# Squared norms of q taken per head behind q's convolution in place of per chunk in the chunk preparation (a DeltaNet and retention block on one core)

## The chip, the core and the metric

The kernel runs on one core of a Trainium2 chip. The core has four compute engines with a queue of their own each: PE (TensorE, matrix products and transposes), DVE (VectorE), ACT (ScalarE) and POOL (GpSimd); a fifth, SP (SyncE), issues DMA transfers, which ACT and POOL issue as well. Each engine works through its own list of instructions in order, and waits on semaphores for data of the others. The metric is the time of one execution on the device in microseconds (us).

## The reference

One layer over 256 context tokens and 1024 latent tokens of width 1024. The input is normalized and modulated, one projection gives the columns of two groups of four heads (a gated DeltaNet, group A, and a retention, group B), the heads' outputs are normalized, gated and projected back, and a SwiGLU follows. The change concerns the norm of q in group A:

```python
def l2_normalize(t):
    return t * lax.rsqrt(jnp.sum(t * t, axis=-1, keepdims=True) + NORM_EPS)
...
    p = (h @ w_in).astype(f32)
...
    qkv_a = jnp.concatenate([short_conv(qkv_a[:, :CTX_LEN], cw), short_conv(qkv_a[:, CTX_LEN:], cw)], axis=1)
    q, k, v = [t.reshape(b, tl, N_HEADS_GDN, HEAD_DIM) for t in jnp.split(qkv_a, 3, axis=-1)]
    q = l2_normalize(q) * (HEAD_DIM ** -0.5)
    k = l2_normalize(k)
...
    o_f = gated_delta_rule(q, k, v, g_f, jax.nn.sigmoid(b_f))
    o_b = to_bwd(gated_delta_rule(to_bwd(q), to_bwd(k), to_bwd(v), to_bwd(g_b), to_bwd(jax.nn.sigmoid(b_b))))
    o_gdn = rms_norm(o_f + o_b, gdn_norm_g) * jax.nn.silu(z.reshape(b, tl, N_HEADS_GDN, HEAD_DIM))
```

The convolution has five taps along the tokens and ends in a SiLU. The output of the delta rule is linear in q, so the kernel leaves q unnormalized and puts the norm into the RMS norm of the output: it needs |q|² for every latent token and head, and only there.

## The kernel before, in words

Tokens are cut into ten tiles of 128 (two of context, t = 0 and 1, and eight latent); heads of group A are 128 wide. All matrix products of the projections are done as three products of a split into high and low parts (`hhi`, `hlo`, `whi`, `wlo`). The order of stages is this.

- *Token-major projections* (`token_major(g, ...)`, matmuls in L371 to L373, bank `tm`): one group g of 256 columns, all tiles in pairs. What comes out goes through one operation (`res`, for rg a SiLU, L532) and to DRAM (`rd`, `zd`, L387).
- *k*, and then *q*: for each of four heads `conv_block` makes the projection with the channels on partitions (L611 to L613, bank `b`, name `b2`), copies it out on ACT (L614, L615), adds the other four taps on DVE (L621) and takes the SiLU on ACT (L624). The head's result `y` (128 channels x 1280 tokens, three buffers) is stored to `kd` or `qd`. For k, `kstat` also transposes each tile of y and sums its squares on ACT (L638). For q only the store follows.
- *rg* is `token_major(6)` and `token_major(7)`.
- *Chunk preparation* `pre(t)`: it loads a tile of k (`kc`) and, for t >= 2, of q (`qc`), both with four heads; takes k kT (`kk`) and, for latent tiles, transposes qc (`qt`, bank `pb`), sums the squares of the transposes into `nq` on ACT (L712), and takes k qT (`kq`). For both directions d it loads a row of decay sums (`gw`, from the product `gr`, L504), masks it on POOL (`e`, L722), takes exponentials on ACT (L726) and multiplies on DVE to `ut` (L730) and `sp` (L732).
- *Inversion* `invert(b)`: 32x32 blocks of three batches of tiles ([0,1,2,9], [3,8,4,7] and [5,6]) are inverted in 31 steps on DVE and POOL (L765 to L767); ACT and DVE copy the blocks to L (L758, L759) first. `merge(b)` joins the blocks with small matmuls (`m`).
- *v*: the same convolution for four heads, then transposes (`vT`), scaled on ACT into `vt` (L859, two buffers) and stored in `sd`.
- The *scan* over tiles in both directions follows; each step and direction loads one `pk` (128 x 3072, 1.5 MB) from `sd`, and has products `kS`, `Tr`, `up` and `o` on PE. Two steps stand ahead of the last projections, the others are interleaved with the retention, which begins with the loads `rdl`, `jcol`, `dist` and `vg` on SP. `gate` uses nq at the end of each tile's scan. Output projection and SwiGLU end the program.

Code order is not the order of execution: a scheduler fixes, when the program is built, the order of each engine's list, and instructions of several stages are mixed in it, as far as buffers allow. So v's first convolutions, the inversions and rg stand between the pieces of the chunk preparation.

PSUM banks are in three pools: `pa` (`tm`, `vT`), `pb` (`kt`, `qt`, `kk`, `kq`, `m`; three banks) and `pc` (the convolutions; two banks).

Of the kernel before, what the change touches and what calls it, by code (L numbers as in the profile page):

```python
# [11 lines left out]
AF = mybir.ActivationFunctionType  # L12
# [5 lines left out]
P = 128  # L18
D = 1024
KT = D // P  # L20
NCTX = 256
# [4 lines left out]
H = 4  # L26
# [12 lines left out]
def build(nc, tc, ap, dbg=None, stop=None, marks=None):  # L39
    root = ExitStack()  # L40
    V, S, G, T, SY = nc.vector, nc.scalar, nc.gpsimd, nc.tensor, nc.sync
# [24 lines left out]
    def checkpoint(name):  # L66
        if dbg is not None:
            marks.append((name, int(nc.cur_bb.bb.instructions[-1].name.split("-")[-1])))
        if stop == name:
            raise Stop()  # L70
# [16 lines left out]
    def bank(tag, name):  # L87
        return PS["pool"].tile([P, 512], F32, tag=tag, name=name, bufs=PS["tags"][tag])
# [4 lines left out]
    def bank_b(name):  # L93
        return bank("pb", name)
# [6 lines left out]
    def const(name, shape):  # L101
        t = C.tile(shape, F32, tag=name, name=name)
        S.dma_start(t, ap[name])
        return t
# [86 lines left out]
    try:  # L191

        cc = const("cc", [P, KT, 2])
        ident = const("ident", [P, P])
# [37 lines left out]
        W2 = None  # L232
# [127 lines left out]
        def tm_weights(g, kh, pl, q=S):  # L360
            return weights(ap["wt"][g, :, 4 * kh:4 * kh + 4, :], [4, 256], V, pl, q, raws.get((g, kh)), g == 0)

        def tm_bank(g):
            return bank_a("tm")[:, 0:WIDE if g == 0 else 256]
# [24 lines left out]
        def token_major(g, tiles, finish, store, pl, q=S):  # L389

            w = [tm_weights(g, kh, pl, q) for kh in range(2)]

            for p in range(0, len(tiles), 2):
                pair = [(t, tm_bank(g)) for t in tiles[p:p + 2]]
                for kh in range(2):
                    for t, o in pair:
                        tm_half(o, w[kh], kh, t)
                for t, o in pair:
                    tm_store(g, t, o, finish, store, pl)
# [47 lines left out]
        W2 = pool("w2", bufs=2)  # L447
# [86 lines left out]
        LAT, ALL = list(range(2, TT)), list(range(2, TT)) + [0, 1]  # L534
# [9 lines left out]
        nq = GS.tile([P, LT, H], F32, tag="nq", name="nq")  # L544
# [81 lines left out]
        def newy():  # L626
            return CV.tile([P, NTOK], F32, tag="y", name="y", bufs=3)
# [27 lines left out]
        for h in range(H):  # L655
            y = newy()
# [17 lines left out]
        sv = rsqrt(GS, nkf, TT * H, "sv")  # L674
        V.tensor_tensor(sv, sv, nkf, ALU.mult)
        sv3 = sv.rearrange("p (t h) -> p t h", h=H)
        for h in range(H):
            y = newy()
            conv_block(h, y, True)
            if h < 2:  # L680
                ada_rest(5, h)
            S.dma_start(qd[:, :, h, :].rearrange("t p j -> p t j"),
                        y[:, NCTX:].rearrange("p (t j) -> p t j", j=P))

        checkpoint("q")
        for g in (6, 7):
            token_major(g, LAT, fin_gate, S, W2, SY)
        checkpoint("rg")
        close(R2)
        close(W2)  # L690
# [9 lines left out]
        def pre(t):  # L700
# [4 lines left out]
                T.matmul(pk[:, h * P:(h + 1) * P], kc[:, h, :], kc[:, h, :], start=True, stop=True)  # L705
            if t >= 2:
                qc = load(GP, qd[t - 2], "qc", 2)
                pn = bank_b("qt")
                for h in range(H):
                    T.transpose(pn[:, h * P:(h + 1) * P], qc[:, h, :], ident)  # L710
                for h in range(H):
                    S.activation(pn[:, h * P:(h + 1) * P], pn[:, h * P:(h + 1) * P], AF.Square, accum_out=nq[:, t - 2, h:h + 1])  # L712
                pq = bank_b("kq")
                for h in range(H):
                    T.matmul(pq[:, h * P:(h + 1) * P], kc[:, h, :], qc[:, h, :], start=True, stop=True)
# [134 lines left out]
        for h in range(H):  # L850
            y = newy()
# [14 lines left out]
        for t in BATCH[2]:  # L866
            pre(t)
# [390 lines left out]
        for i, l in enumerate(pairs):  # L1258
            y = nxt
# [395 lines left out]
```

## Time and profile before

| what | us |
|---|---|
| three runs, in order of size | 1477.37, 1479.93, 1480.02 |
| the profiled execution's own time | 1477.96 |
| its span in the trace | 1476.2 |
| PE, DVE, ACT, POOL busy in the span | 1397.2, 964.6, 614.0, 590.3 |

The page of the profile begins with busy time by engine, then gives the span in 40 slices, the DMA queues, the chain of work that ended last, and the costliest groups of instructions. Of such a group the columns are line, engine and operation, out<-in with partitions x elements, and the count; then busy us and mean ns of one, and the idle time ahead of them on their engine with what ended most of it. The timeline has start, duration, engine (SPq and ACTq are these engines' DMA issues), and in brackets the idle time before with its releaser. A busy PE is not PE at its peak, since matmuls are pipelined: the step from one start to the next tells what one costs. Line numbers are those of the kernel before; the same line stands 10 further down in the changed kernel behind the added function.

### The profile page before, as it was taken

What the parts mean: (1) busy time and instruction counts of PE and PEld (TensorE: products, weight loads), DVE (VectorE), ACT (ScalarE), POOL (GpSimd) and SP (SyncE); (2) the same over time, 40 slices, a digit from 0 to 9 for tenths busy, and PEclk for the clock granted to TensorE, in tenths of its full rate; (3) what the DMA queues carried; (4) which work ended last, traced back from release to release, by engine and by line L of the source; (5) the groups of instructions that cost most, each with busy time, mean ns of one, the idle gap of its engine ahead of it and who ended that gap; (6) DMA issues with size and microseconds to landing.
All of it is one profiled execution on the core that took longest, in us unless ns stands there. A gap on an engine that the chain in (4) does not pass through costs nothing.

```text
span 1476.2 us, 24111 instructions
## 1 busy us (share of the span) xinstructions
PE 1397.2 (95%) x8919; PEld 1199.2 (81%) x8919; DVE 964.6 (65%) x1856; ACT 614.0 (42%) x1326; POOL 590.3 (40%) x501
## 2 busy tenths in 40 slices
PE   7999999986789999899799899999999999999997
PEld 2898888975689999898688688877888888788885
DVE  6566789289792435689676877556555564657477
ACT  5643564587333111245443623233333332444445
POOL 0120010243202344234144688898555552335321
PEclk9999999998899999999899999999999999999999
DMA  9536686688888625996532265674222242776863
GB/s 337 197 105 205 189 249 200 219 264 277 282 216 277 238 76 178 416 341 209 184 125 104 97 238 210 242 264 162 105 97 105 107 151 79 260 260 194 288 216 114
DMA packets 170421, 298.14 MB, mean 202 GB/s; under 512 B 43496, under 2 KB 93880, under 8 KB 165952
## 3 DMA queue, kind: packets, MB, share of 16 engines
q1 hardware_dynamic: 118752, 253.17, 50.2%
q10 hardware_dynamic: 49072, 35.83, 7.8%
q0 software_dynamic: 2480, 7.60, 1.4%
q8 instruction: 70, 1.15, 0.3%
q14 instruction: 47, 0.39, 0.1%
HBM read 206.60 MB, written 89.96 MB: 201 GB/s over the span
## 4 chain that ended last, share of the span: by engine, by line
PE 55%; POOL 6%; DMA 5%; DVE 4%; issue 2%; ACT 2%; SPq 1%; ACTq 0%; POOLq 0%; DVEq 0%
PE ffn L1344 7%; PE ffn L1342 6%; PE ffn L1343 6%; PE fo L1470 4%; PE fo L1469 4%; PE fo L1468 4%; PE tm L371 3%; PE tm L373 3%; PE tm L372 3%; PE op L1203 2%; PE op L1201 2%; PE op L1202 2%; DMA wd<-tw 2%; POOL ws L1315 1%; DMA pk<-sd 1%
## 5 line engine op out<-in xcount | busy, mean ns | idle before, releaser
L371 PE MATMUL tm<-whi,hhi 128*128 128x256 f32 (+1 forms) x704 | 199.5, 287 | 7.7 <-ACT vt L859 3.4
L372 PE MATMUL tm<-wlo,hhi 128*128 128x256 f32 (+1 forms) x704 | 199.3, 285 | 2.4 <-issue 2.0
L373 PE MATMUL tm<-whi,hlo 128*128 128x256 f32 (+1 forms) x704 | 197.7, 285 | 0.0
L371 PEld LDWEIGHTS tm<-whi,hhi 128*128 128x128 f32 x704 | 132.8, 190 | 11.8 <-ACT vt L859 3.6
L1342 PE MATMUL ffn<-t,whi 128*128 128x512 f32 x352 | 136.9, 390 | 1.3 <-ACT whi L344 1.3
L1344 PE MATMUL ffn<-t,wlo 128*128 128x512 f32 x352 | 137.0, 390 | 1.0 <-DVE wlo L345 1.0
L1343 PE MATMUL ffn<-t,whi 128*128 128x512 f32 x352 | 137.0, 389 | 0.0
L372 PEld LDWEIGHTS tm<-wlo,hhi 128*128 128x128 f32 x704 | 133.7, 190 | 2.1 <-issue 0.9
L373 PEld LDWEIGHTS tm<-whi,hlo 128*128 128x128 f32 x704 | 132.8, 190 | 2.6 <-issue 1.8
L344 ACT ACTIVATE whi<-wraw 128x512 fp32r<-128x512 f32 (+2 forms) x98 | 75.1, 771 | 141.4 <-PE ffn L1343 80.5
L344 ACT ACTIVATE whi<-ws 128x512 fp32r<-128x512 f32 x88 | 55.6, 632 | 171.5 <-PE ffn L1343 123.4
L345 DVE TENSOR_TENSOR wlo<-ws,whi 128x512 fp32r<-128x512 f32 x88 | 93.9, 1068 | 47.0 <-ACT whi L344 46.8
L1469 PE MATMUL fo<-wlo,ahi 128*128 128x512 f32 x308 | 120.2, 390 | 2.1 <-DVE wlo L345 2.1
L1468 PE MATMUL fo<-whi,ahi 128*128 128x512 f32 x308 | 119.3, 390 | 0.7 <-ACT ahi L344 0.7
L1470 PE MATMUL fo<-whi,alo 128*128 128x512 f32 x308 | 119.0, 390 | 0.0
L345 DVE TENSOR_TENSOR wlo<-wraw,whi 128x512 fp32r<-128x512 f32 (+2 forms) x92 | 99.4, 1082 | 24.6 <-ACT whi L344 24.6
L1342 PE MATMUL ffn<-b,whi 128*128 128x512 f32 x264 | 103.8, 393 | 4.4 <-ACT whi L344 4.4
L1344 PE MATMUL ffn<-b,wlo 128*128 128x512 f32 x264 | 103.6, 393 | 0.8 <-DVE wlo L345 0.8
L1343 PE MATMUL ffn<-b,whi 128*128 128x512 f32 x264 | 103.4, 392 | 0.0
L612 PE MATMUL b<-hlo,whi 128*128 128x512 f32 (+1 forms) x256 | 94.4, 369 | 0.0
L613 PE MATMUL b<-hhi,wlo 128*128 128x512 f32 (+1 forms) x256 | 94.3, 368 | 0.0
L611 PE MATMUL b<-hhi,whi 128*128 128x512 f32 (+1 forms) x256 | 94.3, 368 | 0.0
(446 smaller groups left out, 3448.1 us busy)
## 6 DMA issues: line engine op xcount, KB each, us to landing
adaw<-ada SPq DMA_DIRECT2D x48, 512.0 KB, 4.4
pk<-sd SPq DMA_DIRECT2D x16, 1536.0 KB, 10.0
wraw<-wfi SPq DMA_DIRECT2D x44, 512.0 KB, 3.7
ar<-ad SPq DMA_DIRECT2D x33, 512.0 KB, 4.7
w<-wfo SPq DMA_DIRECT2D x22, 512.0 KB, 5.7
wd<-tw SPq DMA_DIRECT2D x11, 1024.0 KB, 4.8
ad<-act SPq DMA_DIRECT2D x20, 512.0 KB, 3.0
raw<-wd SPq DMA_DIRECT2D x20, 512.0 KB, 4.9
```

The costliest lines, as they stand in the source:

```text
L344: S.activation(hi, raw, AF.Copy)
L345: e.tensor_tensor(lo, raw, hi.bitcast(F32), ALU.subtract)
L371: T.matmul(o, hhi[:, k, tsl], whi[:, k % 4, :], start=(k == 0), stop=False)
L372: T.matmul(o, hhi[:, k, tsl], wlo[:, k % 4, :], start=False, stop=False)
L373: T.matmul(o, hlo[:, k, tsl], whi[:, k % 4, :], start=False, stop=(k == KT - 1))
L612: T.matmul(o, whi[:, k, :], hl, start=False, stop=False)
L1342: T.matmul(o, whi[:, k, :], xhi(xn, slice(0, 4), k), start=(first and k == 0), stop=False, **kw)
L1343: T.matmul(o, whi[:, k, :], xlo(xn, slice(0, 4), k), start=False, stop=False, **kw)
L1344: T.matmul(o, wlo[:, k, :], xhi(xn, slice(0, 4), k), start=False, stop=(k == 3), **kw)
L1468: T.matmul(po[g][i], ahi[:, ts], whi, start=(j == 0 and not kw), stop=False, **kw)
L1469: T.matmul(po[g][i], ahi[:, ts], wlo, start=False, stop=False, **kw)
L1470: T.matmul(po[g][i], alo[:, ts], whi, start=False, stop=(j == FH - 1), **kw)
```

## The change

The transposes of q and the sums of their squares leave `pre(t)` and go into a new function `qstat(h, y)`. It works on a head at a time, straight from the convolution's result y in SBUF: eight transposes in two banks named `qt`, and eight squares in place in the bank, with the sum to nq. The call for head h - 1 stands behind the convolution of head h, that for the last head between `token_major(6)` and `token_major(7)`. The store to qd and the loads qc stay, since kq and sp use them. The number of transposes (32) and of squares (32) is as before.

```diff
+        def qstat(h, y):
+
+            for l0 in (0, 4):
+                pn = bank_b("qt")
+                for i in range(4):
+                    T.transpose(pn[:, i * P:(i + 1) * P], y[:, NCTX + (l0 + i) * P:NCTX + (l0 + i + 1) * P], ident)
+                for i in range(4):
+                    S.activation(pn[:, i * P:(i + 1) * P], pn[:, i * P:(i + 1) * P], AF.Square,
+                                 accum_out=nq[:, l0 + i, h:h + 1])
+
+        qys = []
         for h in range(H):
             y = newy()
             conv_block(h, y, True)
...
+            qys.append(y)
+            if h:
+                qstat(h - 1, qys[h - 1])
 
         checkpoint("q")
-        for g in (6, 7):
-            token_major(g, LAT, fin_gate, S, W2, SY)
+        token_major(6, LAT, fin_gate, S, W2, SY)
+        qstat(H - 1, qys[H - 1])
+        token_major(7, LAT, fin_gate, S, W2, SY)
...
                 qc = load(GP, qd[t - 2], "qc", 2)
-                pn = bank_b("qt")
-                for h in range(H):
-                    T.transpose(pn[:, h * P:(h + 1) * P], qc[:, h, :], ident)
-                for h in range(H):
-                    S.activation(pn[:, h * P:(h + 1) * P], pn[:, h * P:(h + 1) * P], AF.Square, accum_out=nq[:, t - 2, h:h + 1])
                 pq = bank_b("kq")
```

The scheduler makes a new order of every engine's list from it. Three places matter for what follows. The first is ACT around the SiLU of q's last head (L624, y 128x1024). Before, it stands ahead of the first exponentials (e, L726):

```order
L614 ACTIVATE u<-b_3545 128x256
L615 ACTIVATE y<-b_3545,cw 128x256
L624 ACTIVATE y<-y 128x1024
L532 ACTIVATE res<-tm 128x256
L682 DMA qd<-y 128x8x128
```

In the changed kernel (e is L736, the new squares are L684):

```order
L736 ACT_TABLE_LOAD
L736 ACTIVATE e<-e,nG 128x128
L684 ACTIVATE qt,nq<-qt 128x128
L736 ACTIVATE e<-e,nG 128x128 x3
L387 DMA rd<-res 128x256
L684 ACTIVATE qt,nq<-qt 128x128
L624 ACT_TABLE_LOAD
L624 ACTIVATE y<-y 128x1024
L684 ACTIVATE qt,nq<-qt 128x128 x3
L693 DMA qd<-y 128x8x128
```

The SiLU has moved behind eight exponentials (four more stand just above these rows) and has a table load of its own, and squares of the head before stand between.

The second place is ACT behind the SiLU of v's last head, where vT is scaled into vt and stored. Before, ACT's copy for the second inversion (L758) stands behind all of vt:

```order
L859 ACTIVATE vt<-vT,svy 128x128 x2
L860 DMA sd<-vt 128x2x128
L859 ACTIVATE vt<-vT,svy 128x128 x4
L860 DMA sd<-vt 128x4x128
L859 ACTIVATE vt<-vT,svy 128x128 x4
L860 DMA sd<-vt 128x4x128
L532 ACTIVATE res<-tm 128x256
L387 DMA zd<-res 128x256
L758 ACTIVATE L<-yr 64x1024
```

In the changed kernel (the copy is L768, vt L869):

```order
L869 ACTIVATE vt<-vT,svy 128x128 x2
L870 DMA sd<-vt 128x2x128
L869 ACTIVATE vt<-vT,svy 128x128 x4
L870 DMA sd<-vt 128x4x128
L768 ACTIVATE L<-yr 64x1024
L532 ACTIVATE res<-tm 128x256
L387 DMA zd<-res 128x256
L869 ACTIVATE vt<-vT,svy 128x128 x4
```

The copy has moved ahead of the last four vt.

The third place is SP's queue where the projections end and the retention begins. L664 is the line of `load`, so the tile names tell the loads apart. Before:

```order
L664 DMA pk_7070<-sd 128x3072
L664 DMA pk_7082<-sd 128x3072
L993 DMA rdl<-rdl 128x8
L995 DMA jcol<-jcol 128x2
L664 DMA dist<-dist 128x256
L664 DMA vg<-rd 128x2x512 x4
L664 DMA zg<-zd 128x512 x2
```

In the changed kernel:

```order
L1003 DMA rdl<-rdl 128x8
L1005 DMA jcol<-jcol 128x2
L664 DMA dist<-dist 128x256
L664 DMA vg<-rd 128x2x512 x4
L664 DMA pk_7070<-sd 128x3072
L664 DMA pk_7082<-sd 128x3072
L664 DMA zg<-zd 128x512 x2
```

The two loads pk of one scan step have moved from ahead of rdl to behind the four vg.

## The prediction

> **What bounds the kernel now.** I read the page's head first, then busy time by stretches, then the waits and the timeline of PE (TensorE), ACT and DVE where PE has gaps, and the chain of waits there. The head of the page:
>
> ```profile
> span 1476.2 us, 24111 instructions
> PE 1397.2 (95%) x8919; PEld 1199.2 (81%) x8919; DVE 964.6 (65%) x1856; ACT 614.0 (42%) x1326; POOL 590.3 (40%) x501
> ```
>
> PE is the bound of the program as a whole, so time comes from its gaps alone. The view by stretches gives start and end, the length, the busy time of PE, PE's weight loads, DVE, ACT and POOL, then the granted clock, the DMA share and GB/s.
>
> ```profile
> 259.00:296.00 37.00, 37.00 (x265) 33.91 (x264) 10.70 (x15) 22.40 (x61) 10.10 (x14) 1.00 0.69 221
> 296.00:391.00 95.00, 70.26 (x425) 61.26 (x424) 80.07 (x127) 68.93 (x191) 38.32 (x32) 0.91 0.87 276
> 570.00:580.00 10.00, 10.00 (x87) 10.00 (x86) 2.88 (x12) 0.00 (x0) 4.29 (x9) 1.00 0.15 53
> 580.00:640.00 60.00, 54.60 (x452) 52.92 (x451) 42.67 (x160) 19.70 (x51) 18.50 (x21) 0.97 0.96 372
> 590.00:600.00 10.00, 8.60 (x74) 8.22 (x74) 9.96 (x31) 2.41 (x5) 4.23 (x4) 1.00 1.04 419
> ```
>
> Where the rg projection ends and the first kk run (259 to 296 us) PE has no gap. From 296 to 391 us (v convolutions between the chunk preparations) PE idles 95.0 - 70.3 = 24.7 us, while DVE is busy 80 and ACT 69 of 95 us. From 580 us (start of the interleaved scan) PE idles 5.4 us of 60 and the DMA engines are full (share 0.96, 1.04 at its worst), though just before, at 570 us, they are nearly idle (0.15). The change works in these three places.
>
> **Part 1: transposes and squares go in among the q convolutions and rg.** PE gets 32 more transposes where it has no gap. The closest operation it ran is the transpose of k for its norms (kstat). PE's timeline (start, duration, instruction) shows ten of those and the matmul behind them, then the end of q's last convolution and the spacing of a projection's and a convolution's matmuls:
>
> ```profile
> 161.28 1.25 PE L638 MATMUL kt<-ident,y 128*128 128x128 f32 x10
> 162.29 0.36 PE L611 MATMUL b<-hhi,whi 128*128 128x256 f32 x1
> 243.26 0.28 PE L371 MATMUL tm<-whi,hhi 128*128 128x256 f32 x1
> 247.09 0.28 PE L613 MATMUL b<-hhi,wlo 128*128 128x256 f32 x1
> 247.21 0.28 PE L611 MATMUL b<-hhi,whi 128*128 128x256 f32 x1
> ```
>
> Ten take 162.29 - 161.28 = 1.01 us, so 32 take 3.2 us. In exchange the new order moves 24 matmuls of 256 columns (0.12 us each, by the last two starts) and 11 of 512 (twice the columns, so about 0.24 us, an estimate from the same rows) of the first v head from before the first kk to behind it: 2.9 + 2.6 = 5.5 us.
>
> One wait is new. The transposes of q head 3 stand in PE's order only 43 instructions ahead of the first kk, with rg's last matmuls queued behind them, and they need that head's SiLU. ACT now runs this SiLU behind eight exponentials of the chunk preparation, a projection's SiLU, squares of the head before, and three table loads; in the trace it stood ahead of all of them. ACT's and DVE's timelines (in brackets the idle time before and what ended it):
>
> ```profile
> 257.17 1.06 ACT L624 ACTIVATE y<-y 128x1024 f32<-128x1024 f32 x1 [6.29 <-DVE y L621]
> 261.10 0.68 DVE L505 TENSOR_TENSOR row<-row,gr 1x512 f32<-1x512 f32 x1 [1.84 <-PE gr L504]
> 268.53 2.46 ACT L726 ACTIVATE e<-e,nG 128x128 f32<-128x128 f32 x8 [1.46 <-POOL e L722]
> 277.48 1.29 DVE L730 TENSOR_TENSOR ut<-kk,e 128x512 f32<-128x512 f32 x2 [15.70 <-POOL X L755]
> 289.01 0.26 ACT L712 ACTIVATE qt<-qt 128x128 f32<-128x128 f32 x1
> 289.41 0.26 ACT L712 ACTIVATE qt<-qt 128x128 f32<-128x128 f32 x1
> 306.03 1.28 ACT L726 ACT_TABLE_LOAD   x1
> 307.32 1.28 ACT L726 ACTIVATE e<-e,nG 128x128 f32<-128x128 f32 x4
> ```
>
> The exponentials hang on the gate rows, which hang on the matmul gr. In the new order gr stands 90 matmuls of 256 columns behind the point at 243.3 us: 243.3 + 90 x 0.12 = 254, some 6 us ahead of DVE's use of it at 261 in the trace, and the exponentials, at 268.5 there, come 6 us earlier, at about 262.5. From then ACT needs 2.5 (eight exponentials) + 3 x 1.28 (tables) + 0.4 (the projection's SiLU, taken like a square) + 4 x 0.40 (squares, by the two starts at 289) + 1.1 (head 3's SiLU) = 9.4 us, so this SiLU ends near 272 and not at 258. PE gets to the transposes after 97 matmuls and 24 transposes more: 254 + 0.5 + 97 x 0.12 + 2.4 = 268.5. It waits about 3 us. First kk: 3.2 + 3 - 5.5 = +1 us, and 5.5 us of v convolution are left to run inside the 24.7 us of gaps, which cover them. Without that cover they would cost 5.5. I take 0, with bounds of -2 (exponentials and kk come early and PE waits for nothing) and +6 (the wait is twice as long, behind a late gate row, and nothing covers it).
>
> Here a page speaks against the change. The Trainium skill, "ScalarE: Activation LUTs", section "What ACT_TABLE_LOAD costs", gives a switch of table 1283 ns and another 1380 ns for ACT to drain. In the trace the exponential starts 0.01 us behind the end of the 1.28 us load, so I see no drain; with it the three switches would add 4.1 us to PE's wait, an estimate from that page.
>
> **Part 2: the v stage loses them.** PE's 3.2 us of transposes leave a stretch with gaps, so they win nothing by themselves. What do the squares win? The group of the squares (busy us, mean ns of one, idle before):
>
> ```profile
> L712 ACT ACTIVATE qt<-qt 128x128 f32<-128x128 f32 x25 | 6.8, 274 | 0.9 <-ACT qt L712 0.8
> ```
>
> These 25 of the 32 behind 296 us, with their accumulator reads, hold ACT 25 x 0.27 to 25 x 0.40 = 7 to 10 us. But who sets the end of the stage? It ends with the transposes of the last v head. First the DVE timeline (the copy behind the first inversion's early steps, the last tap), and a small tap; then the chain of waits there:
>
> ```profile
> 254.79 0.48 DVE L621 SCALAR_TENSOR_TENSOR y<-u,cw,y 128x254 f32<-128x254 f32 x1
> 311.99 1.47 DVE L759 COPY L<-yr 64x1024 f32<-64x1024 f32 x1
> 370.34 1.27 DVE L621 SCALAR_TENSOR_TENSOR y<-u,cw,y 128x1022 f32<-128x1022 f32 x1
> ```
>
> ```profile
> 372.44 1.28 ACT L624
> 375.06 0.70 PE vT L856 x2
> ```
>
> And the waits between 215 and 460 us (sum, count, longest) and two groups of DVE:
>
> ```profile
> DVE ut L730 <- ACT e L726: 7.0, 4, 3.7
> L767 DVE TENSOR_TENSOR X<-X,tmp 128x31 f32<-128x31 f32 (+23 forms) x93 | 35.0, 376 | 2.7
> L732 DVE TENSOR_TENSOR sp<-kq,e 128x512 f32<-128x512 f32 x13 | 8.7, 677 | 0.0
> ```
>
> From the copy at 312 to the last tap at 370 us DVE is hardly idle, so it sets the pace; ACT does so only where DVE waits for an exponential, 7.0 us in all, of which I count 5 as gained since some would wait for POOL's part anyway. Against that the new order of DVE puts more ahead of the last tap: three small taps before the copy (3 x 0.48 = 1.4) and behind it one more small tap (0.5), three products ut and sp (3 x 0.68 = 2.0) and four inversion steps (4 x 0.38 = 1.5): 5.4 us. Net 0, with bounds of -10 (ACT is the bound after all and all its relief counts) and +5.4 (nothing is won). No load goes away: qd is still stored, and qc is still read for kq.
>
> Then one thing gets better. ACT's copy of L for the second inversion no longer stands behind the last four vt, which wait for a store of vt's buffer. The timeline of ACT and DVE, then two pieces of the chain of waits:
>
> ```profile
> 385.83 1.14 ACT L859 ACTIVATE vt<-vT,svy 128x128 f32<-128x128 f32 x4 [7.78 <-DMA sd<-vt]
> 389.32 0.20 DVE L765 TENSOR_TENSOR tmp<-L,X 128x31 f32<-128x31 f32 x1 [5.03 <-ACT L L758]
> ```
>
> ```profile
> 438.79 2.19 issue
> 461.39 1.25 issue
> ```
>
> DVE starts that inversion up to 5.0 us sooner; PE gains only what it waits at the two later merges, at most 2.19 + 1.25 = 3.4 us. I take -1.5, with bounds of 0 and -3.4.
>
> **Part 3: a pair of scan loads moves behind the end of the projections.** This term decides. In the new order of SP's queue the pair of pk loads that stood ahead of rdl stands behind rdl, jcol, dist and four vg. SP's timeline and PE's first state products; then the DMA issues from 550 to 640 us (count, KB each, median us to landing); then the chain of waits:
>
> ```profile
> 555.05 2.34 SPq L664 DMA_DIRECT2D pk<-sd  x2
> 582.08 4.13 SPq L664 DMA_DIRECT2D vg<-rd  x4
> 588.47 1.95 PE L914 MATMUL kS<-S,pk 128*128 128x128 f32 x16
> ```
>
> ```profile
> pk<-sd SPq DMA_DIRECT2D x10, 1536.0 KB, 10.9
> vg<-rd SPq DMA_DIRECT2D x15, 512.0 KB, 9.8
> ```
>
> ```profile
> 591.43 15.38 DMA pk<-sd
> 606.86 1.86 PE kS L914 x8
> ```
>
> Now two loads of 1.5 MB go out at 555 us into idle DMA engines. rdl and what follows it take their buffers from the projections and go out only when these end; the four vg end the queue's row at 582 + 4 = 586 us, and there the pair would go out, into the stretch with share 1.04. Its 3.15 MB at the 419 GB/s of that stretch are 7.5 us. PE uses the pair at 588.5; with the 2.1 MB of the four vg ahead, 5.2 MB from 582 on land by 582 + 12.5 = 594.5 or a little later. That is 6 to 7 us late, of which other products can fill some. The next pair, for which PE now waits till 606.86 behind a load of 15.4 us, lands up to 7.5 us later, since nothing frees the queue before 640 (share 0.96). I take +6, with bounds of 0 (PE's 5.4 us of gaps in this stretch swallow it) and +9 (7.5, and 1.5 where the step's products, now ahead of its transposes, hold these up too).
>
> **Sum**: 0 + 0 - 1.5 + 6 = +4.5 us. The profiled execution took 1477.96 us, so 1482.5; the median of the three runs, 1479.93, lies 2.0 above it, so 1484 us against that median.
>
> **Rivals.**
> - *ACT is the bound of the v stage.* For it: ACT is busy 69 of 95 us there, and the last head's SiLU (L624), with its table load, stands in the chain right ahead of 375. Against it: DVE's 80 us. It gives -10 in place of 0 in part 2, so -5.5 in all: 1474; with the loads hidden too, 1468.
> - *The pair of loads is hidden.* For it: the pair is used over some microseconds, and PE has other matmuls to run. Against it: the share of 1.04. It gives 0 in place of +6, -1.5 in all: 1478. That the squares cost nothing where they go and save nothing counts with it.
> - *The v stage gets later.* If exponentials are awaited as before, 5.4 us of DVE work come on top of part 3, and decide as soon as DVE's waits shrink by less than 5 us: 4.5 + 5.4 = +10: 1490.
>
> **How the numbers follow.** Forecast 0.45 (its own range 1480 to 1489); ACT the bound 0.24; hidden loads 0.18; later v stage 0.13. A measurement of this kernel cannot tell less than about 0.2%, 3 us, from no change. Slower by more: the forecast but for its lowest part (0.38) and the later v stage (0.13), 0.51. Faster by more: most of the first rival (0.21) and the low end of the second (0.04), 0.25. Within: 0.24. The range, 1472 to 1491, leaves out the far end of the first rival and of the last, less than 2 in 10.
>
> **What would show it.** Part 1: a gap of PE of about 3 us at the transposes of q head 3, between 265 and 275 us, and the first kk at 275 to 279. Part 2: the last head's vT between 373 and 379 us, and PE's gaps from 296 to 391 near 24 us. If those transposes come before 370, ACT was the bound and I am wrong. At the second inversion DVE's wait of 5.0 us for L goes. Part 3: the pair goes out behind vg, PE stands at kS for 4 to 8 us near 590, and the stretch from 580 to 640 us has 10 us of PE gaps in place of 5.4. If those stay at 5, the loads were hidden.

## The result: 11 us slower, where 4.5 were forecast

| | median, us | runs, lowest to highest |
|---|---|---|
| before, same chip | 1479.88 | 1477.37 to 1480.02 |
| changed kernel | 1490.94 | 1488.0 to 1494.03 |
| ratio | 1.0081 | 95% interval 1.0060 to 1.0103 |

A second series of the changed kernel on another occasion gave 1.0060 (1.0041 to 1.0078). The profiled execution of the changed kernel has a span of 1486.2 us against 1476.2.

The head of its page, and the stretches that the prediction read, in the same columns:

```profile
span 1486.2 us, 24119 instructions
PE 1403.4 (94%) x8919; PEld 1204.2 (81%) x8919; DVE 967.6 (65%) x1856; ACT 616.5 (41%) x1328; POOL 589.8 (40%) x501
```

```profile
259.00:296.00 37.00, 33.96 (x246) 32.76 (x245) 12.20 (x16) 29.82 (x107) 8.82 (x12) 0.91 0.50 161
296.00:391.00 95.00, 71.92 (x403) 62.38 (x403) 81.21 (x126) 65.02 (x145) 36.66 (x31) 0.89 0.86 276
580.00:640.00 60.00, 53.37 (x442) 51.08 (x441) 35.64 (x133) 16.62 (x38) 17.27 (x22) 1.00 0.89 348
```

The first row is new: PE was never idle from 259 to 296 us, and now it lacks 3.0 us there and runs at a granted clock of 0.91. The second and third rows hardly differ from before. But stretches at fixed times hide a shift, so I cut both traces at the same instructions of PE: *front* from the last of the column sums (`gr<-ones`) that stands ahead of q's end (217.3 us before) to the first kk; *v stage* from there to the last vT group; *merges and scan* from there to the first matmul of the output projection; *rest* is all else. Each number is the difference of two starts in PE's timeline, each column one profiled execution. The second profiles of both kernels (before2, after2 below) tell how far such a length repeats.

| us | before | before2 | changed | after2 | difference of the means |
|---|---|---|---|---|---|
| front | 59.0 | 59.7 | 64.6 | 64.8 | +5.35 |
| v stage | 98.8 | 100.0 | 102.1 | 100.8 | +2.05 |
| merges and scan | 338.7 | 337.9 | 338.4 | 343.3 | +2.55 |
| rest | 979.7 | 981.4 | 981.0 | 980.6 | +0.25 |
| span | 1476.2 | 1479.0 | 1486.2 | 1489.5 | +10.2 |

So about half of the time arises in front, where the prediction had put nothing, and no stage behind it takes it back. The 2.05 us of the v stage are little more than the 1.2 and 1.3 by which two profiles of one kernel differ there, but seven more kernels with the change (further down) have 100.2 to 103.1 us. The 2.55 us of merges and scan come from after2 alone, which is 4.9 us above the other profile of the same kernel, and no cost is shown there.

**Front.** PE's timeline of the changed kernel has two waits there that the kernel before has not, and then the first kk:

```profile
250.21 0.39 PE L372 MATMUL tm<-wlo,hhi 128*128 128x256 f32 x1 [1.52 <-DVE wlo L345]
275.59 1.12 PE L682 MATMUL qt<-ident,y 128*128 128x128 f32 x4 [3.04 <-ACT qt L684]
283.37 1.95 PE L720 MATMUL kk<-kc 128*128 128x128 f32 x16
```

The second wait, 3.04 us at the transposes of q's last head, is the one forecast. It ends 1.2 us behind the end of the SiLU (274.41), with a square that frees the bank. ACT's timeline shows what it stands behind, exponentials and three table loads:

```profile
265.62 1.28 ACT L736 ACTIVATE e<-e,nG 128x128 f32<-128x128 f32 x4 [0.28 <-POOL e L732]
267.20 1.28 ACT L532 ACT_TABLE_LOAD   x1
268.49 0.39 ACT L532 ACTIVATE res<-tm 128x256 f32<-128x256 f32 x1
268.90 1.28 ACT L736 ACT_TABLE_LOAD   x1
272.06 1.28 ACT L624 ACT_TABLE_LOAD   x1
273.35 1.06 ACT L624 ACTIVATE y<-y 128x1024 f32<-128x1024 f32 x1
```

Not forecast was what comes behind the wait. In steps of 2 us (the last three columns are granted clock, DMA share and GB/s):

```profile
272.00:274.00 2.00, 0.55 (x5) 0.35 (x3) 0.00 (x0) 1.97 (x3) 0.00 (x0) 1.00 0.00 0
274.00:276.00 2.00, 0.41 (x2) 0.41 (x3) 0.00 (x0) 2.00 (x13) 0.00 (x0) 0.67 0.28 89
276.00:278.00 2.00, 2.00 (x11) 2.00 (x10) 0.00 (x0) 2.00 (x13) 0.00 (x0) 0.50 0.73 238
278.00:280.00 2.00, 2.00 (x11) 2.00 (x11) 0.00 (x0) 1.16 (x7) 0.00 (x0) 0.50 0.66 215
280.00:282.00 2.00, 2.00 (x13) 2.00 (x13) 0.00 (x0) 1.48 (x8) 0.00 (x0) 0.62 0.34 116
282.00:284.00 2.00, 2.00 (x19) 2.00 (x19) 0.00 (x0) 0.77 (x2) 0.40 (x1) 1.00 0.22 75
```

The clock falls to a half for some 6 us; busy time times what the clock lacks is 2.9 us. The sum of the front is 3.2 (transposes) + 3.0 + 1.5 (waits) + 2.9 (clock) - 5.5 (convolution moved out) = 5.1 us; the lengths give 5.35. In the second profile the wait is 3.9 and the clock takes 1.5.

**v stage.** ACT has less to do, and much of it becomes idle time. From the first kk to the last vT, what ACT's and DVE's exponentials wait for, before and now (sum, count, longest):

```profile
ACT e L726 <- POOL e L722: 11.7, 9, 2.6
DVE ut L730 <- ACT e L726: 7.0, 4, 3.7
```

```profile
ACT e L736 <- POOL e L732: 18.9, 8, 4.3
ACT y L624 <- DVE y L621: 6.7, 3, 3.6
DVE ut L740 <- ACT e L736: 6.7, 2, 6.2
```

In this pair of profiles DVE waits for exponentials as long as it did, 6.7 us against 7.0, and ACT waits longer for POOL's mask of the same tile (18.9 against 11.7). The second profiles, before2 and after2, agree on the mask (11.2 and 20.0) but not on DVE's wait:

```profile
DVE ut L730 <- ACT e L726: 12.0, 6, 3.8
DVE ut L740 <- ACT e L736: 7.2, 3, 5.8
```

There 4.8 us were gained, so what DVE gained lies between 0.3 and 4.8 us. The end of the stage, in the timelines:

```profile
382.01 1.28 ACT L624 ACT_TABLE_LOAD   x1 [0.43 <-ACT vt L869]
382.80 1.27 DVE L621 SCALAR_TENSOR_TENSOR y<-u,cw,y 128x1022 f32<-128x1022 f32 x1
385.43 2.40 PE L866 MATMUL vT<-ident,y 128*128 128x128 f32 x10 [13.66 <-ACT y L624]
391.38 0.21 DVE L775 TENSOR_TENSOR tmp<-L,X 128x31 f32<-128x31 f32 x1
```

From the first kk (276.29 before, 283.37 now) to the last tap it was 94.0 us and is 99.4. That these are the 5.4 us that the prediction had counted on DVE is luck to this digit: in the second profiles the stretch grew from 95.3 to 98.2, by 2.9. ACT gives 2.1 back between the tap and vT, in both pairs alike: before, the SiLU's table load began at 372.44, behind a scaling and a square and 0.8 us behind the tap's end; now it is over when the tap ends. PE's gaps of this stage are still there (the 13.66 us ahead of the last vT is one). DVE's wait of 5.0 us for L at the second inversion is gone (last row).

**Scan.** SP and PE in the changed kernel:

```profile
590.10 1.64 SPq L664 DMA_DIRECT2D pk<-sd  x2
602.88 0.91 PE L924 MATMUL kS<-S,pk 128*128 128x128 f32 x6 [1.41 <-DMA pk<-sd]
```

The pair goes out behind vg as forecast, but PE's longest wait for a pk is 1.41 us (1.81 in after2; before it was 1.12), not 4 to 8, and its gaps from 580 to 640 us are 6.6 us in place of 5.4, not 10.

### The profile page after: what moved, and what is told of

It reads as the page before. It is cut to its first block, busy times and chain, and to the rows that moved or that the text cites. A ratio compares the mean times of both kernels' runs of the same rounds, so it can differ in the third digit from the quotient of the medians.

```text
span 1486.2 us, 24119 instructions
## 1 busy us (share of the span) xinstructions
PE 1403.4 (94%) x8919; PEld 1204.2 (81%) x8919; DVE 967.6 (65%) x1856; ACT 616.5 (41%) x1328; POOL 589.8 (40%) x501
## 4 chain that ended last, share of the span: by engine, by line
PE 55%; DMA 7%; POOL 6%; DVE 4%; issue 3%; ACT 3%; SPq 1%; ACTq 0%; POOLq 0%; DVEq 0%
PE ffn L1354 6%; PE ffn L1352 6%; PE ffn L1353 6%; PE fo L1478 5%; PE fo L1480 5%; PE fo L1479 5%; PE tm L371 3%; PE tm L373 3%; PE tm L372 3%; PE op L1213 2%; PE op L1211 2%; PE op L1212 2%; DMA wd<-tw 1%; POOL ws L1325 1%; PE up L939 1%
## 5 line engine op out<-in xcount | busy, mean ns | idle before, releaser
L345 DVE TENSOR_TENSOR wlo<-wraw,whi 128x512 fp32r<-128x512 f32 (+2 forms) x92 | 102.6, 1117 | 26.7 <-ACT whi L344 26.4
```

The source lines that it names most:

```text
L345: e.tensor_tensor(lo, raw, hi.bitcast(F32), ALU.subtract)
```

## The experiments

Each ratio is against the kernel before on the same chip. The lengths are cut as in the table above; means of the two profiles for the two kernels are 59.35 / 99.4 / 338.3 before and 64.7 / 101.45 / 340.85 changed. A length comes from one execution, a ratio from the median of several: the execution with the profile lay between 5.6 us below that median (nvt3) and 4.2 us above it (bnosq2, against bnosq), and what is outside the three stages took from 975.5 (bd20) to 983.4 us (late). So lengths tell where an edit acts, and do not add up to the ratio in their row. The lengths of pklate and bnosq are those of their repeats, pklate2 and bnosq2; bnosq2 is a single execution and has no ratio.

| run | what | ratio (95%) | front | v stage | merges and scan |
|---|---|---|---|---|---|
| noq3 | changed, last head left out | 1.0046 (1.0024 to 1.0067) | 62.5 | 102.2 | 342.0 |
| late | changed, last head behind rg | 1.0058 (1.0043 to 1.0073) | 63.4 | 100.2 | 337.1 |
| bankc | changed, last head in other banks | 1.0065 (1.0042 to 1.0088) | 61.9 | 101.8 | 341.5 |
| tponly | changed, no squares | 1.0056 (1.0039 to 1.0072) | 63.3 | 102.5 | 341.8 |
| silu1st | changed, SiLU ahead of exponentials | 1.0061 (1.0040 to 1.0082) | 60.1 | 102.6 | 347.9 |
| scr | changed, squares into SBUF | 1.0033 (1.0021 to 1.0045) | 59.9 | 103.1 | 339.1 |
| avt3 | changed, third vt buffer | 1.0026 (1.0007 to 1.0046) | 63.5 | 102.6 | 334.3 |
| pklate | before, pk pair behind vg | 1.0065 (1.0043 to 1.0087) | | | |
| pklate2 | the same again | 1.0044 (1.0028 to 1.0060) | 59.5 | 99.3 | 345.5 |
| bd20 | before, 20 matmuls added in front | 1.0057 (1.0039 to 1.0076) | 63.6 | 98.8 | 344.3 |
| bdum | before, 30 matmuls added in front | 1.0080 (1.0064 to 1.0096) | 67.0 | 101.2 | 341.4 |
| vlate | before, v convolution behind kk | 1.0076 (1.0053 to 1.0098) | 56.9 | 107.9 | 343.4 |
| bnosq | before, no squares, no transposes | 1.0023 (1.0008 to 1.0037) | | | |
| bnosq2 | the same again, for its profile | | 59.8 | 95.4 | 349.0 |
| nvt3 | bnosq and a third vt buffer | 1.0007 (0.9989 to 1.0024) | 59.2 | 94.4 | 343.5 |
| bvt3 | before, third vt buffer | 1.0059 (1.0038 to 1.0079) | 59.2 | 98.7 | 345.6 |

**Does a delay in front reach the end, or do gaps take it?** Matmuls are added behind rg, 30 in bdum and 20 in bd20:

```diff
             token_major(g, LAT, fin_gate, S, W2, SY)
-        checkpoint("rg")
+        dum = bank_b("dum"); [T.matmul(dum, hhi[:, 0, 0:P], hhi[:, 0, 256:768], start=True, stop=True) for _ in range(30)]; checkpoint("rg")
```

> The kernel before with 30 matmuls of 512 columns added right ahead of the first kk (their result is not used), so PE works 30 x 0.233 = 7.0 us longer there without a gap and the first kk comes 7 us later; the pair of pk loads also falls behind vg. Theory A (the v stage is a chain that starts at the first kk and passes a delay on): last vT 6 to 7 us later, total +7 to +9, 1487 to 1489. Theory B (24.7 us of gaps cover it): last vT within 2 us of 375, total +1 to +3 from the loads alone, or +6 if the prediction's price of the loads holds: then pklate shows it too.

> The kernel before with 20 added matmuls of 512 columns (result not used) right ahead of the first kk: 4.7 us more PE work there, and, other than with 30 of them, SP's order is that of before with the pk pair ahead of rdl, and PE's order of the scan that of before too. Theory A (a delay in front is passed on one to one, and the changed scan order costs some 4 us of its own): +4.7, ratio 1.003, where 30 gave 1.008. Theory C (delays in front grow, the scan order costs nothing): 20 thirtieths of what 30 cost, +8, 1.0053. Theory B (gaps cover the front): +0 to +1.

PE's timeline of the kernel before, and that of bd20:

```profile
276.29 1.95 PE L705 MATMUL kk<-kc 128*128 128x128 f32 x16
375.06 2.39 PE L856 MATMUL vT<-ident,y 128*128 128x128 f32 x10 [9.27 <-ACT y L624]
```

```profile
281.02 1.95 PE L705 MATMUL kk<-kc 128*128 128x128 f32 x16
379.83 2.40 PE L856 MATMUL vT<-ident,y 128*128 128x128 f32 x10 [9.05 <-ACT y L624]
```

The first kk is 4.7 us later and the last vT 4.8: the v stage passes a delay on whole, though PE has 20 us of gaps in it. With 30 matmuls, too, the front is 7.7 us longer and the v stage (101.2) no shorter. That step of the prediction is refuted. The total, +8 (1.0057), was theory C's number, but not by its mechanism: the delay does not grow on its way to vT. Where the 8 us lie this profile does not show: its execution was 4.6 us longer than the mean of before's two. Merges and scan are 6 us longer in it, with 12 us of PE's work lost to a low clock ahead of the first state update against 3 and 9 in the two profiles of before, and the stretches outside of the three stages are 5 us shorter.

**Is the last head's wait the cause in front?** Three runs take it out in different ways.

```diff
         token_major(6, LAT, fin_gate, S, W2, SY)
-        qstat(H - 1, qys[H - 1])
         token_major(7, LAT, fin_gate, S, W2, SY)
+        qstat(H - 1, qys[H - 1])
...
-                pn = bank_b("qt")
+                pn = bank_c("qt") if h == H - 1 else bank_b("qt")
```

The first of these edits is late; with its removed line alone it is noq3, where nq of that head is a constant. The last is bankc.

> The changed kernel without the transposes and squares of q's last head (its nq is a constant; the other three heads are as in the change), so nothing stands ahead of the last rg matmuls that needs the last head's SiLU; the order up to the merges is otherwise that of the changed kernel, and the pk loads stay behind the four vg. Theory A (the loss arises in front: PE's 3.0 us wait at these transposes, the low granted clock behind it, about 3 us, and all that follows starts that much later): first kk at about 276 to 277 and not 283.4, the last vT some 6 us earlier than the changed kernel's 385, total 1483 to 1486 against the 1490.9 of the changed kernel. Theory B (the prediction: gaps of the v stage cover the front, the scan loads cost 6 us): first kk early as well, but the last vT and the total as in the changed kernel, 1490 within 2.

> The changed kernel with the last head's transposes and squares called behind both rg groups, not between them: the same work, and the eight transposes stand right ahead of the first kk with all rg matmuls ahead of them. Theory A: PE reaches them at about 276.5 when the SiLU (274.4) is done, no wait, no low clock; first kk 277.5, total 1484 to 1487. Theory B: 1490 within 2, since neither the loads' order nor the v stage changes.

> The changed kernel with the transposes of q's last head in the two banks of the convolutions, which are free there, not in the three that the other heads' squares hold; all eight stand together, everything else keeps its order. If the wait of 3.0 us is for a bank that the squares hold (squares go on 1 us behind the SiLU), it shrinks to about 1.5 to 2 us and total is 1 to 3 us below the changed kernel (1.006 to 1.0075); if it is for the SiLU itself, it stays near 3 and total stays at 1.008.

Their ratios, 1.0046 to 1.0065, are not clear of the changed kernel's two (1.0060 and 1.0081), and their fronts are still 2.5 to 4 us longer than before's. (In noq3 one load of the pk pair is back ahead of rdl and the order of the merges is another, so its total tests more than the edit.) PE's timeline of noq3 says why:

```profile
275.32 0.38 PE L371 MATMUL tm<-whi,hhi 128*128 128x256 f32 x1 [2.92 <-ACT res L532]
```

With the transposes gone, the next rg matmul waits 2.92 us in their place, for a bank that ACT's `res` has not read out. It does so in late, too. In bankc the wait is for the SiLU itself (2.85 us), so the bank was not the reason either. PE waits there for ACT's queue, whatever stands next.

**Are the squares what fills ACT's queue?**

In tponly they are left out, and nq is a constant:

```diff
-                for i in range(4):
-                    S.activation(pn[:, i * P:(i + 1) * P], pn[:, i * P:(i + 1) * P], AF.Square,
-                                 accum_out=nq[:, l0 + i, h:h + 1])
```

> The changed kernel without the 32 squares (the transposes stay in their new place, nq is a constant); the orders of PE's v stage and scan, of DVE and of SP are those of the changed kernel, ACT's is the same less the squares. Theory D (in front ACT's queue is what PE waits for: res and the SiLU stand there behind exponentials, table loads and squares, and the granted clock halves behind PE's gap): the wait of 2.9 to 3.0 us near 273 goes, with it the low clock; first kk at 277 to 278 (32 transposes cost 3.2 us, the moved convolution gives 5.5 back, the wait for wlo 1.5 stays), total 1482 to 1485, ratio 1.003 to 1.0045 against 1.008. If it is the transposes or the order of the v stage and not the squares, the ratio stays at 1.007 to 1.008.

```profile
272.10 1.82 PE L683 MATMUL qt<-ident,y 128*128 128x128 f32 x8 [2.72 <-ACT y L624]
```

Theory D falls: without a single square PE waits 2.72 us for the SiLU. What is left ahead of it in ACT's queue are the exponentials, a projection's res and the table loads. So the order was set:

```diff
-            S.activation(y[:, a0:], y[:, a0:], AF.Silu)
+            silu.append(S.activation(y[:, a0:], y[:, a0:], AF.Silu).ins)
...
-                    S.activation(e[:, h, :], e[:, h, :], AF.Exp, bias=sm["nG"][:, col:col + 1])
+                    with (tc.issue_after(silu[7]) if t < 2 else nullcontext()): S.activation(e[:, h, :], e[:, h, :], AF.Exp, bias=sm["nG"][:, col:col + 1])
```

> The changed kernel with one order set: ACT's first exponentials of the chunk preparation wait in its queue for the SiLU of q's last head; the eight exponentials, res and squares around it move a little, all of DVE's, SP's and the later ACT and PE orders stay those of the changed kernel. Theory E (PE's wait of 3 us in front is ACT's order, exponentials and table loads ahead of SiLU and res, whatever the squares do, and the half clock behind it is part of its price): no wait near 273, first kk 4 to 5.5 us earlier relative to the last gr (stretch 59 to 60.5 against 64.6), v stage as long as in the changed kernel (102), total 1485 to 1487, ratio 1.0045 to 1.0055. If the v stage had absorbed the front, the total would stay at that of the changed kernel.

```profile
279.40 1.95 PE L720 MATMUL kk<-kc 128*128 128x128 f32 x16
381.97 2.40 PE L866 MATMUL vT<-ident,y 128*128 128x128 f32 x10 [13.69 <-ACT y L624]
```

The wait goes and the front is 60.1 us, 4.6 shorter, with squares and transposes all in place: theory E holds for the front. The v stage keeps its 102.6. The total did not follow: merges and scan took 347.9 us, 4.6 to 9.5 more than in the two profiles of the changed kernel, and the ratio is that of the changed kernel on this occasion (1.0060). Part of the 347.9 is this one execution, 2.9 us above the run's median, in which PE lost 11 us of its work to a low clock ahead of the first state update, against 6 and 9 in the changed kernel. So what the front's 4.6 us are worth at the end of the program is not shown.

**Squares into SBUF.** The same squares write to a scratch tile; the order then comes out with the SiLU early and the pk pair in front.

```diff
+                qsc = R2.tile([P, 512], F32, tag="qsc", name="qsc", bufs=2)
...
-                    S.activation(pn[:, i * P:(i + 1) * P], pn[:, i * P:(i + 1) * P], AF.Square,
+                    S.activation(qsc[:, i * P:(i + 1) * P], pn[:, i * P:(i + 1) * P], AF.Square,
```

> The changed kernel with the squares written to a scratch tile in SBUF, not in place in the bank (0.25 us apart in kstat's squares, 0.40 in place), for which the order comes out with the last head's SiLU and transposes earlier and with the pk pair ahead of rdl as in the kernel before; PE's order of the scan is that of before but for 10 rows. Theory A: no wait at the last head's transposes, first kk some 2 us later than before (32 transposes, less the v convolution that moved), scan as before: +1 to +3, ratio 1.001 to 1.002. Theory C: +2 to +4. The prediction's theory (loads decide): 0 to -1.5, since the pair is back in front.

```profile
257.45 0.28 ACT L685 ACTIVATE qsc<-qt 128x128 f32<-128x128 f32 x1 [2.33 <-PE qt L683]
...
257.72 0.27 ACT L685 ACTIVATE qsc<-qt 128x128 f32<-128x128 f32 x1
```

The front is 59.9, 0.5 above before's mean; the v stage is 103.1, 3.7 longer; 1.0033 in all, somewhat more than theory A's 1.001 to 1.002. The change can thus be had at little cost in front, and it still loses. Against the changed kernel the early SiLU and the pk pair in front come together here, so the run does not tell which of them the gain is due to.

**What lengthens the v stage?** In the kernel before, only v's first convolution is held behind the first kk:

```diff
-                    T.matmul(o, whi[:, k, :], hh, start=(k == 0), stop=False)
+                    with (tc.issue_after(kk0[0]) if b == 8 else nullcontext()): T.matmul(o, whi[:, k, :], hh, start=(k == 0), stop=False)
...
-                T.matmul(pk[:, h * P:(h + 1) * P], kc[:, h, :], kc[:, h, :], start=True, stop=True)
+                kk0.append(T.matmul(pk[:, h * P:(h + 1) * P], kc[:, h, :], kc[:, h, :], start=True, stop=True).ins)
```

> The kernel before (norms of q in the chunk preparation) with v's first convolution held behind the first kk, as it stands in the changed kernel: 24 matmuls of 256 and 11 of 512 columns move, 5.5 us. The order of the scan also comes out with the pk pair behind vg. The prediction's step (what moves behind the first kk runs in the v stage's gaps): front 53 to 54 us, v stage 99 as before, so the last vT 5.5 us earlier. Theory F (v's convolution heads the chain of the v stage: what is not done ahead of the first kk lengthens it): front 53 to 54, v stage 103 to 105, last vT within 1.5 us of before.

```profile
252.16 0.39 PE L372 MATMUL tm<-wlo,hhi 128*128 128x256 f32 x1 [2.61 <-DVE wlo L345]
275.85 1.95 PE L706 MATMUL kk<-kc 128*128 128x128 f32 x16
383.73 2.39 PE L857 MATMUL vT<-ident,y 128*128 128x128 f32 x10 [14.26 <-ACT y L624]
```

Theory F holds, and more: the front gives back only 2.4 us, because the convolution had covered a wait for rg's weights (2.61 us, and 1.52 in the changed kernel), and the v stage is 8.5 us longer for 5.5 us of matmuls. v's convolution is no filler there; it heads the chain from copy over taps and SiLU to vT. The ratio, 1.0076, is no price of this move alone, since SP's new order also has the pk pair behind vg, which cost 1.0044 and 1.0065 by itself (pklate below).

**What are the squares worth where they were?** In bnosq and bnosq2 they are left out together with their transposes, and nq is a constant.

```diff
-                pn = bank_b("qt")
-                for h in range(H):
-                    T.transpose(pn[:, h * P:(h + 1) * P], qc[:, h, :], ident)
-                for h in range(H):
-                    S.activation(pn[:, h * P:(h + 1) * P], pn[:, h * P:(h + 1) * P], AF.Square, accum_out=nq[:, t - 2, h:h + 1])
```

> The kernel before without the transposes and squares of q altogether (nq is a constant): what the chunk preparation gains by losing them, with nothing added in front. The prediction's reading (DVE paces the v stage): 0 to -2 us, last vT within 2 us of 375. The rival (ACT is the bound): -7 to -10, last vT at 365 to 368.

> The kernel before without the transposes and squares of q once more, for its profile: by the times of its first run (ratio 1.0023) the chunk preparation gains nothing from losing them. If DVE paces the v stage, the stretch from the first kk to the last vT is 97 to 99 us as before (98.8); if ACT does, 89 to 92 us, and the time is lost again later.

```profile
377.49 0.37 ACT L855 ACTIVATE vt<-vT,svy 128x128 f32<-128x128 f32 x1 [1.45 <-DMA sd<-vt]
390.96 1.14 ACT L855 ACTIVATE vt<-vT,svy 128x128 f32<-128x128 f32 x4 [12.34 <-DMA sd<-vt]
```

```profile
392.16 0.58 PE L371 MATMUL tm<-whi,hhi 128*128 128x256 f32 x1 [8.01 <-ACT vt L855]
```

The v stage is 4.0 us shorter than before's mean, between the two expectations. Whether it is the squares on ACT or the transposes on PE that gave way the run cannot tell, since both are gone. And yet the kernel is no faster: the last vt now waits 12.34 us for the store of its buffer (7.78 before), PE stands 8.01 us behind it (3.38 before), and merges and scan take 349.0. A third buffer was tried in three kernels.

```diff
-                vt = CV.tile([P, 4, P], F32, tag="vt", name="vt", bufs=2)
+                vt = CV.tile([P, 4, P], F32, tag="vt", name="vt", bufs=3)
```

> The kernel before without the transposes and squares of q (nq is a constant), as in the run bnosq, and with a third buffer for vt, so that the last four scaled transposes need not wait for a store. Theory G (losing the squares shortens the v stage by 4 us, and the wait of 12.3 us of the last vt for its store, and the 8.0 us PE gap behind it, swallow that and more): v stage 95 to 97, merges 109 to 114 against 122, total 2 to 6 us below bnosq's 1481 to 1486, at or below the kernel before: ratio 0.998 to 1.000. If the merges stay above 118, the store is not what swallows it.

> The kernel before with a third buffer for vt and nothing else. In its trace the last vt waits 7.8 us for the store, and PE has a gap of 3.4 us there. Theory G: 0 to 3 us faster, ratio 0.998 to 1.000. If the buffer does not matter: within 0.2%, or slower by the merges' order.

> The changed kernel with a third buffer for vt. Its last vt waits 1.7 us for the store, so theory G gives little here: 0 to 2 us below the changed kernel, ratio 1.005 to 1.008; front 64 to 65 us as in the changed kernel.

```profile
389.65 0.39 PE L371 MATMUL tm<-whi,hhi 128*128 128x256 f32 x1 [2.61 <-ACT res L532]
```

Theory G did not come out. In nvt3 the buffer takes both waits away and PE's longest wait there is 2.61 us. But the merges, from the last vT to the first state update, still take 120.2 us against 122.1, above the 118 that the expectation had set: the store is not what swallows the gain. The ratios of nvt3 and bnosq, 1.0007 and 1.0023, are not clear of each other, and that of nvt3 is as before's with 32 transposes and squares less. In the kernel before, the buffer made things 9 us slower, where theory G had 0 to 3 us faster; in the changed kernel it made them 5 to 8 us faster, against its 0 to 2. In both, PE's new order differs in hundreds of rows of the v stage and the merges, and in avt3 the pk pair stands ahead of rdl again, so the buffer is not what was measured there. None of these kernels beats the one before.

**What does the pk pair cost?**

```diff
-            SY.dma_start(x, src)
+            loads.setdefault(tag, []).append(SY.dma_start(x, src).ins)
...
-            pk = load(PK, sd[t, :, 4:4 + n] if d == 0 else sd[t, :, 6 - n:6], "pk%d" % d, 2, (P, n, 512))
+            with tc.issue_after(loads["vg"][3]) if s == 4 else nullcontext():
+                pk = load(PK, sd[t, :, 4:4 + n] if d == 0 else sd[t, :, 6 - n:6], "pk%d" % d, 2, (P, n, 512))
```

> The kernel before with one change: the pair of pk loads of the scan's fifth step is issued behind the four vg, as in the changed kernel; everything ahead of the scan is as before. Theory A (the loads cost little): 1481 to 1482 (+1 to +2), gaps of PE from 580 to 640 us 6 to 7 us against 5.4. Theory B (the prediction's term): +6, 1486, with 10 us of gaps there.

> The kernel before with the one pair of pk loads behind the four vg once more, for its profile. If the loads cost what the three times of the first run say (+7 to +10), the stretch from the first state product of the scan to the output projection is 7 to 10 us longer than the 229.7 us of before; if the changed kernel's trace is right, where that stretch is 230.1 with the pair behind vg, it is within 2 us of 229.7 and the time elsewhere.

```profile
588.96 1.29 SPq L664 DMA_DIRECT2D pk<-sd  x2
```

```profile
597.39 1.16 PE L1028 MATMUL ru<-vg,kz 128*128 128x128 f32 x8 [3.84 <-POOL kz L1024]
```

In the kernel before, the pair behind vg costs what the prediction said: 1.0044 and 1.0065 are 6.5 and 9.6 us, and merges and scan are 7.2 us longer. PE's gap is not at kS but at ru, 3.84 us, a wait for POOL's kz. In the kernel before, kS and Tr of the pair stood ahead of ru (kS at 588.47, ru at 592.89) and ran while kz was made; in pklate2 ru stands ahead of them. The changed kernel's order has kS, Tr, up and o of another step there (kS at 588.39, ru at 598.67), so that PE is busy until kz is done. Its merges and scan are 2.55 us longer and no more.

**How far does a profile repeat?**

> The kernel before once more, for a second profile: how far the lengths of its stages (front 59.0, v stage 98.8, merges 109.0, scan 229.7, up to the feed-forward 113.3, tail 249.5 us) repeat from one execution to the next. If PE's low clock behind gaps is a matter of the order alone, each repeats within 0.5 us; if it also depends on when in some window the gap falls, stages with gaps of 2 to 3 us differ by 2 to 6 us.

> The changed kernel once more, on the same chip as the others, for a second profile and a tighter ratio. If the attribution by stages holds, front 64 to 65 us, v stage 101.5 to 103, merges 107 to 111, scan 229 to 231, and ratio 1.007 to 1.0085; if the front's low clock was chance, the front is 61.5 to 62.

The lengths above show it: front within 0.7 us, v stage within 1.3, merges and scan within 0.8 in one kernel and 4.9 in the other. Much of the last is clock: PE's busy time lost to a low clock between vT and the scan's first state update is about 3 and 9 us in the two profiles of before, 6 and 9 in those of the changed kernel.

## Why the prediction was wrong

The sign and the reason for the front's wait were right, the size was not: +4.5 forecast, about +10 in the traces and +11 in the medians. The sign itself was partly luck, since it hung on the +6 of the loads, and the time came from elsewhere. By its steps:

- *Part 1, "5.5 us of v convolution are left to run inside the 24.7 us of gaps, which cover them"*: this is the step that failed: the gaps cover nothing. The front came out at +5.35 and not at the +1 worked out, and the v stage covered none of it and was itself 2.05 longer. The wait of 3 us was sized rightly (3.0 and 3.9). Missing were the half clock behind it (2.9 and 1.5 us) and the wait for rg's weights (1.5) that the moved convolution had covered. And the gaps of the v stage lie ahead of vT, at the end of the chain that starts with kk and v's convolution; bd20 shows a delay passed on one to one, vlate that the convolution is on that chain.
- *Part 2, "7.0 us in all, of which I count 5 as gained"*: 6.7 us remained in the first pair of profiles, a gain of 0.3, but 7.2 of 12.0 in the second, a gain of 4.8; the 5 are neither shown nor refuted. Much of ACT's freed time went into waiting for POOL's masks. The other side, 5.4 us more ahead of the last tap, came out as 5.4 and 2.9. The stage grew by 2.05; vlate's +8.5 and bnosq2's -4.0 would make +4.5, so the parts do not simply add. This is the rival in which the v stage gets later, and its time, 1490, is the one that came. Its other half, 6 us from the loads, was too much and the front's 5.35 stood in for it.
- *Part 2, second inversion*: the wait for L went, as said. Whether PE gained the 1.5 us can't be read off, because the merges scatter by more.
- *Part 3, "+6"*: the price was right for the kernel before (pklate), and too high for the changed one, where merges and scan together lost 2.55, no more than its two profiles differ by. What was missed is that the new order of PE's products puts those of another step where the pair is awaited.
- *The rival in which ACT is the bound of the v stage* has at most 4.0 us to it (bnosq2, where PE's transposes go as well), and they did not reach the end of the program (1.0023).

What stays open: why a new order of the list, with the same work, moves merges and scan between 334 and 349 us. The low clock accounts for part of it; the store of vt, whose wait is gone in nvt3, does not. Which order is good was not found out. Nor is it shown that the program gets shorter when the front does: silu1st took 4.6 us out of the front, and its ratio stayed at 1.0061. A run with the clock held up through the wait in front was not tried.

## What to carry to other kernels

Ask of a gap whether the work that moves could run in it: idle time at the end of a chain does not cover a delay at the chain's start, and twenty added matmuls ahead of the stage tell it in one run. When work moves to a place where PE is full, count what it pushes out, whether that was filler or the head of a chain, and what it had been covering. Where each edit makes a new order of the whole program, price an edit only against other kernels whose order is alike, and by stages cut at the same instructions.

## What the runs showed of the hardware

PE's granted clock often halves behind a wait of about 3 us, so such a wait costs up to twice its length: 3.04 us were followed by 2.9 us lost, 3.9 us in the second profile by 1.5, 2.85 us in bankc by nothing (clock 1.00 in all four steps from 270 to 278 us), and 2.72 us in tponly by 1.5 (clock 0.57 in both steps from 272 to 276 us). So the length of the wait alone does not decide it. The Trainium skill, "TensorE: Matmul & The Clock Gate", section "HAM oscillation — how this bites in real kernels", warns of PE gaps over some 3.4 us; here 2.92 us (late, noq3) already brought the clock down to 0.50, and 2.72 us to 0.57.

A square that ACT writes in place in a bank came 0.28 to 0.40 us behind the one before, one that it writes to SBUF 0.25 to 0.27 us (scr). And the third table load in front was followed by its SiLU 0.01 us after its end, as the prediction had read it: no extra drain was seen.
